# A hybrid encoder block on one core: six pairs instead of four by seven products, sums of weights on GpSimd, transposes in turns of eight

## The chip, the cores and the metric

The kernel runs on one core of a Trainium2 chip. The metric is the device time of one execution in microseconds (us), the median of some runs. Engines are named as in the profile: PE is the matrix engine (PEld its weight loads), DVE the vector engine, ACT the scalar engine, POOL is GpSimd, SP issues most DMAs.

## The reference

One encoder layer over 256 tokens of 2048 features, all in float32:

```python
h = rms_norm(x, attn_norm)
qa, ka, va, qb, kb, vb, ga, gb = split(h @ w_in)
ya = windowed_gqa(qa, ka, va, table, sink)         # 8 heads, |i-j| <= 128
yb = dilated_attention(qb, kb, vb, table)          # 3 groups of 4 heads
merged = sigmoid(ga) * (ya @ w_branch_a) + sigmoid(gb) * (yb @ w_branch_b)
x = x + merged @ w_out
hf = rms_norm(x, ffn_norm)
g = dwconv_centred(hf @ w_ffn_gate, conv_w, conv_b)  # width 3 along the tokens
x = x + (gelu(g) * (hf @ w_ffn_up)) @ w_ffn_down     # 5632 wide
x = x + sigmoid(rms_norm(x, ple_norm) @ w_ple_gate) * (p @ w_ple_proj)
return rms_norm(x, final_norm)
```

## The kernel before, in words

**Numbers.** A float32 factor is split into two parts that PE takes at full speed: `hi`, a rounded copy (ACT), and `lo`, the rest (DVE, a subtraction). A product is then three matmuls, hi by hi, hi by lo and lo by hi. For weights this is done in `split_to` (L205): a sub-piece of `raw` becomes `whi` (L217) and `wlo` (L218), four buffers each, and each product asks for splits three sub-pieces ahead of its own.

**Weights.** `_plan` lists the jobs, `_stream` the 128x128 weight blocks in the order in which the jobs use them. They lie in memory in pieces of 16 blocks (1 MB), which SP loads one after the other into three `raw` buffers (`load`, L195). A load waits until the piece three before it has been split.

**Stages.** Attention projections and attention; `ga`, `gb`, `ba`, `bb` (gates and branch projections) by quarters of the columns; `o` (`w_out`); then twice, for each half of the 5632 MLP features, `g` and `u` (gate and up projection, by 128 features) and `d0` or `d1` (down projection); `pp` and `pg` (the embedding and its gate), and the last norm. Accumulators lie in PSUM under the tags `acc` (three buffers), `sp`, `pt` (two each) and `misc`.

**The down projection.** A half has 22 blocks of 128 features, taken as 11 pairs. A product covers 1024 columns, so a pair has a 2x2 block matrix of activations (two features blocks by two token halves) and one of weights (two feature blocks by two column halves of 512). Eight small products would do; `seven_product` (L288) does the first `SAVED` pairs by seven, after Winograd's form of Strassen's scheme. Each small product is three matmuls of 512 columns (L311 to L313). `ORDER` mixes pairs by seven with pairs by eight. The seven need sums of weights, `combine` (L222, three DVE subtractions per piece of weights, L229, L233, L234, into the tile `spare`), and sums of activations, `add_up` (L704), made once for all `SAVED` pairs of a half into `shl`. A piece of a pair by seven is split in four parts: two blocks of raw, two of sums. When the last pair by seven is through, `spread_sums` (L721) adds the products `p1`, `p5`, `p6`, `p7` to the residual; the others are added at the end of the product by `joined` (L772).

**Transposes.** Activations are transposed on PE into a `pt` tile, four 128x128 transposes per tile, between the matmuls of another job: `merge` (L761) for the merged branches, `flip` (L740) after `w_out` and after `d1`. `at((job, step), f, ...)` names the place, and `run_due` runs it there.

**The end.** `finish` (L795) sums the squares of a token half (L798), takes the root (`root`, L384: a scaling on DVE and a power on POOL), and scales and stores the rows.

**What sets the order.** Each engine has its own queue in order. The order in a queue is that of a planner in the framework, which goes by the program's order as priority and by its own estimate of when an instruction can run; it also makes all semaphores.

Of the kernel before, what the change touches and what calls it, by code (L numbers as in the profile page):

```python
# [16 lines left out]
P = 128  # L17
T = 256
# [92 lines left out]

ORDER = [4, 0, 5, 1, 6, 2, 7, 3, 8, 9, 10]
SAVED = 4

# [43 lines left out]
def _encoder(ctx: ExitStack, tc, xt, pt, cols, table, onehot, mask, ident_in, last_gain, wts, xrows, out):  # L158
# [32 lines left out]

    raws, subs = {}, {}
    state = {"raw": 0, "sub": 0, "at": 0}

    def load(r, a=0, b=PIECE):  # L195
        if a == 0:
            raws[r] = wpool.tile([P, PIECE, P], F32, name="raw", bufs=3)
        nc.sync.dma_start(raws[r][:, a:b, :], wts[r].rearrange("p (b n) -> p b n", n=P)[:, a:b, :])
        state["raw"] = r + 1
# [5 lines left out]
    def split_to(i):  # L205
        while state["sub"] < min(i, len(_SUBS)):
            s = state["sub"]
            a, n, part = _SUBS[s]
            r, o = divmod(a, PIECE)
            load_all(r + 3)  # L210
            src = raws[r][:, o:o + n, :]
            if part is not None:
                src = combine(src, part)
                n = src.shape[1]
            hi = wpool.tile([P, n, P], FR, name="whi", bufs=4)
            lo = wpool.tile([P, n, P], FR, name="wlo", bufs=4)
            nc.scalar.activation(hi, src, AF.Copy)  # L217
            nc.vector.tensor_tensor(lo, src, hi.bitcast(F32), op=ALU.subtract)  # L218
            subs[s] = (hi, lo)
            state["sub"] = s + 1  # L220

    def combine(b, part):  # L222

        if part == 0:
            state["turn"] = turn = 1 - state.get("turn", 1)
            state["t"] = held["spare"][:, turn * PIECE * P:(turn + 1) * PIECE * P].rearrange("p (b n) -> p b n", n=P)
            four = b.rearrange("p (q b) n -> p q (b n)", q=4)
            t13 = state["t"][:, :8, :].rearrange("p (q b) n -> p q (b n)", q=2)
            nc.vector.tensor_tensor(t13, four[:, 1::2], four[:, :2], op=ALU.subtract)  # L229
            return b[:, 8:, :]  # L230
        if part == 1:
            t1, t2, t4 = (state["t"][:, c:c + 4, :] for c in (0, 8, 12))
            nc.vector.tensor_tensor(t2, b[:, 12:, :], t1, op=ALU.subtract)  # L233
            nc.vector.tensor_tensor(t4, b[:, 8:12, :], t2, op=ALU.subtract)  # L234
            return state["t"][:, :8, :]
        return state["t"][:, 8:, :] if part == 2 else b[:, :4, :]

# [50 lines left out]
    def seven_product(i, still, sums, tags, done):  # L288
# [30 lines left out]
        for m in ORDER:  # L319
            b = state["at"]  # L320
            s, _ = _SUB_OF[b]
            if m < SAVED:
                each = ([("p3", sums(m, 3), 0, 4), ("p2", a(2 * m + 1, 0), 0, 0)],
                        [("p5", sums(m, 0), 1, 0), ("p7", sums(m, 2), 1, 4)],
                        [("p6", sums(m, 1), 2, 0), ("p4", a(2 * m + 1, 1), 2, 4)],
                        [("p1", a(2 * m, 0), 3, 0)])
# [109 lines left out]
    tot = sc.tile([P, T], F32, name="tot")  # L436
    hba = big.tile([P, QH, AW], F32, name="hba", tag="b0", bufs=1)
    hbb = big.tile([P, BH, BW], F32, name="hbb", tag="b1", bufs=1)
    oh = ap_.tile([NBUCK, 2 * T], F32, name="oh", tag="near", bufs=2)
# [184 lines left out]
    def after(job, i, acc, u=None):  # L624
# [66 lines left out]
        elif kind == "u":  # L691
            u = gather(acc)
            nc.vector.scalar_tensor_tensor(u, u, 0.5, rt[1], op0=ALU.mult, op1=ALU.mult)
            f = n % FHALF
            v = held["a32"][:, f, :] if f < 2 * SAVED else u
# [8 lines left out]
    def add_up():  # L704

        a = held["a32"].rearrange("p (m e) (t n) -> p m e t n", e=2, t=2)
        a11, a12, a21, a22 = a[:, :, 0, 0], a[:, :, 1, 0], a[:, :, 0, 1], a[:, :, 1, 1]
        s = held["s32"]
        nc.vector.tensor_tensor(s[:, 0], a21, a22, op=ALU.add)
        nc.vector.tensor_tensor(s[:, 1], s[:, 0], a11, op=ALU.subtract)  # L710
        nc.vector.tensor_tensor(s[:, 2], a11, a21, op=ALU.subtract)
        nc.vector.tensor_tensor(s[:, 3], a12, s[:, 1], op=ALU.subtract)
        hi, lo = held["shl"][:, 0], held["shl"][:, 1]
        for c in (slice(0, 2), slice(2, 4)):
            nc.scalar.activation(hi[:, c], s[:, c], AF.Copy)
            nc.vector.tensor_tensor(lo[:, c], s[:, c], hi[:, c].bitcast(F32), op=ALU.subtract)

# [3 lines left out]
    def spread_sums(n, bank):  # L721
# [14 lines left out]
        add(v, bank["p5"], v)  # L736
        add(q[0][1], u, q[0][1])
        add(q[1][1], v, q[1][1])

# [21 lines left out]
    def merge(n, e, m):  # L761
# [5 lines left out]
        k = 4 * n + 2 * e  # L767
        hi, lo = (held["merged"][k // SUB][:, k % SUB:k % SUB + 2, c:c + T] for c in (0, T))
        nc.scalar.activation(hi, p, AF.Copy)
# [13 lines left out]
    def gate(n, t, acc, last):  # L783
# [9 lines left out]
        return u  # L793

    def finish(t, tail):  # L795

        s = sc.tile([P, 2], F32, name="sum")[:, :1]
        nc.vector.tensor_reduce(s, held["ss3"][:, t, :], axis=AX.X, op=ALU.add)  # L798
        r = root(s, 1)
        whole = res[:, t, :]  # L800
# [10 lines left out]
    def fetch(t, c):  # L811
# [8 lines left out]
    stills = {  # L820
        "o": lambda k: held["merged"][k // SUB][:, k % SUB, :], "ba": lambda k: yab[:, k, :],
        "bb": lambda k: yab[:, QH + k, :], "pp": lambda k: held["ps"][:, k, :], "pg": lambda k: held["pl"][:, k, :],
# [4 lines left out]
    for i, job in enumerate(_JOBS):  # L827
# [4 lines left out]
        if kind == "gb" and n == 0:  # L832
            held["merged"] = [big.tile([P, SUB, 2 * T], FR, name="merged", tag=a, bufs=1) for a in ("b0", "b1")]
        if kind == "o" and n == 0:
# [7 lines left out]
        if kind == "g" and n == 0:  # L842
            spare = held["spare"] = big.tile([P, KC * T], F32, name="spare", tag="b0", bufs=1)
            held["a32"] = spare[:, :2 * SAVED * T].rearrange("p (k t) -> p k t", t=T)
            held["s32"] = spare[:, 2 * SAVED * T:4 * SAVED * T].rearrange("p (e m n) -> p e m n", e=4, n=P)
            held["shl"] = big.tile([P, 2, 4, SAVED, P], FR, name="shl", tag="b1", bufs=1)
# [14 lines left out]
        if kind == "bb":  # L861
            for e in range(2):
                at((i + 1, 3 + 3 * e), merge, n, e, held["m"])
        if kind == "o":
            for e, j in enumerate(((i + 1, 2), (i + 1, 4)) if n < QUARTERS - 1 else ((i + 1, 9), (i + 1, 11))):
                at(j, flip, 4 * n + 2 * e, held["hf"], 1)
        if kind == "d1":
            for e, j in enumerate(((i + 2, 0), (i + 3, 0), (i + 3, 1), (i + 4, 1)) if n else
                                  [(i + 1, k) for k in (17, 18, 19, 20)]):
                at(j, flip, 8 * n + 2 * e, held["pl"], 2)  # L870
        if kind == "pp" and n == 0:
            end = ff.tile([P, 3 * QUARTERS, W4], F32, name="end", tag="act")
            held["ph"] = end[:, :2 * QUARTERS].rearrange("p (t n) w -> p t n w", t=2)
            held["lg"] = end[:, 2 * QUARTERS:].rearrange("p n w -> p (n w)")
        if kind == "pp" and n == 2:
            keep(nc.scalar.dma_start(held["lg"], last_gain))
            nc.vector.tensor_scalar(held["half"], root(rowsums(held["ss2"]), 2), 0.5, None, op0=ALU.mult)
# [48 lines left out]
        elif kind == "pg":  # L926
            for t in range(2):
# [3 lines left out]
                if last:  # L931
                    finish(t, tail)
        else:
            after(job, i, acc)
# [49 lines left out]
```

## Time and profile before

| | us |
|---|---|
| median of 3 runs (1477.53 to 1480.88) | 1478.37 |
| the profiled execution | 1477.88 |
| its span, first to last instruction | 1476.1 |
| PE busy | 1462.2 |
| DVE busy | 1065.5 |
| ACT busy | 760.5 |
| POOL busy | 3.7 |

The profile is one execution. Busy time is the time in which an engine had an instruction under way; in groups, "busy, mean ns of one" stands before the second bar, and after it the idle time of the engine just before these instructions, with what ended it. Matmuls overlap each other, so their mean duration is longer than their pitch.

### The profile page before, as it was taken

What the parts mean: (1) busy time and instruction counts of PE and PEld (TensorE: products, weight loads), DVE (VectorE), ACT (ScalarE), POOL (GpSimd) and SP (SyncE); (2) the same over time, 40 slices, a digit from 0 to 9 for tenths busy, and PEclk for the clock granted to TensorE, in tenths of its full rate; (3) what the DMA queues carried; (4) which work ended last, traced back from release to release, by engine and by line L of the source; (5) the groups of instructions that cost most, each with busy time, mean ns of one, the idle gap of its engine ahead of it and who ended that gap; (6) DMA issues with size and microseconds to landing.
All of it is one profiled execution on the core that took longest, in us unless ns stands there. A gap on an engine that the chain in (4) does not pass through costs nothing. (4 is left out here: it accounts for less than half of the span.)

```text
span 1476.1 us, 19530 instructions
## 1 busy us (share of the span) xinstructions
PE 1462.2 (99%) x7570; PEld 1248.4 (85%) x7570; DVE 1065.5 (72%) x1530; ACT 760.5 (52%) x1072; POOL 3.7 (0%) x9
## 2 busy tenths in 40 slices
PE   9999999999999999999999999999999999999997
PEld 8888888888888888888888888888888888888886
DVE  7686664664554555568898888887889888898565
ACT  7465444444444444555555555554555555655643
POOL 0000000000000000000000000000000000000000
PEclk9999999999999999999999999999999999999998
DMA  9644444445555554545455454555455454555552
GB/s 321 245 156 171 169 171 171 171 177 194 204 197 192 202 207 180 198 171 197 178 196 196 180 196 171 205 223 192 183 196 189 184 198 172 201 200 216 211 188 97
DMA packets 46375, 282.88 MB, mean 192 GB/s; under 512 B 5124, under 2 KB 9988, under 8 KB 14028
## 3 DMA queue, kind: packets, MB, share of 16 engines
q1 hardware_dynamic: 44268, 277.31, 50.8%
q10 hardware_dynamic: 2016, 4.33, 1.1%
q8 instruction: 59, 0.97, 0.2%
q14 instruction: 32, 0.26, 0.0%
HBM read 279.49 MB, written 2.14 MB: 191 GB/s over the span
## 5 line engine op out<-in xcount | busy, mean ns | idle before, releaser
L218 DVE TENSOR_TENSOR wlo<-raw,whi 128x1024 fp32r<-128x1024 f32 (+2 forms) x519 | 622.1, 1201 | 355.6 <-ACT whi L217 352.4
L217 ACT ACTIVATE whi<-raw 128x1024 fp32r<-128x1024 f32 (+2 forms) x519 | 541.1, 1043 | 605.5 <-PE acc L269 224.9
L244 PE MATMUL acc<-mov,whi 128*128 128x512 f32 x1840 | 641.9, 393 | 0.3 <-DVE mov L368 0.3
L245 PE MATMUL acc<-mov,wlo 128*128 128x256 f32 x1840 | 512.8, 279 | 0.0
L244 PEld LDWEIGHTS acc<-mov,whi 128*128 128x128 f32 x1840 | 344.7, 187 | 77.6 <-DVE mov L368 0.6
L245 PEld LDWEIGHTS acc<-mov,wlo 128*128 128x128 f32 x1840 | 346.7, 188 | 0.4
L268 PE MATMUL acc<-wlo,mov 128*128 128x512 f32 (+1 forms) x512 | 196.5, 384 | 0.5 <-DVE wlo L218 0.5
L267 PE MATMUL acc<-whi,mov 128*128 128x512 f32 (+1 forms) x512 | 196.8, 385 | 0.0
L269 PE MATMUL acc<-whi,mov 128*128 128x512 f32 (+1 forms) x512 | 196.4, 384 | 0.0
L267 PEld LDWEIGHTS acc<-whi,mov 128*128 128x128 f32 x512 | 96.7, 189 | 19.3 <-DVE wlo L218 0.8
L268 PEld LDWEIGHTS acc<-wlo,mov 128*128 128x128 f32 x512 | 96.7, 189 | 19.0 <-DVE wlo L218 0.9
L269 PEld LDWEIGHTS acc<-whi,mov 128*128 128x128 f32 x512 | 96.7, 189 | 18.8
L312 PE MATMUL acc<-wlo,act 128*128 128x512 f32 x272 | 106.3, 391 | 0.8 <-DVE wlo L218 0.8
L311 PE MATMUL acc<-whi,act 128*128 128x512 f32 x272 | 106.1, 390 | 0.0
L313 PE MATMUL acc<-whi,act 128*128 128x512 f32 x272 | 105.9, 389 | 0.0
L312 PEld LDWEIGHTS acc<-wlo,act 128*128 128x128 f32 x272 | 51.1, 188 | 12.0 <-DVE wlo L218 1.7
L311 PEld LDWEIGHTS acc<-whi,act 128*128 128x128 f32 x272 | 51.1, 188 | 10.7
L313 PEld LDWEIGHTS acc<-whi,act 128*128 128x128 f32 x272 | 51.1, 188 | 10.5
L267 PE MATMUL acc<-whi,merged 128*128 128x512 f32 x128 | 50.6, 396 | 0.0
L269 PE MATMUL acc<-whi,merged 128*128 128x512 f32 x128 | 49.9, 390 | 0.0
L268 PE MATMUL acc<-wlo,merged 128*128 128x512 f32 x128 | 49.8, 389 | 0.0
L217 ACT ACTIVATE whi<-spare 128x1024 fp32r<-128x1024 f32 x32 | 33.7, 1054 | 27.0 <-PE acc L313 26.2
(177 smaller groups left out, 1373.0 us busy)
## 6 DMA issues: line engine op xcount, KB each, us to landing
raw<-in_wts SPq DMA_DIRECT2D x251, 1024.0 KB, 4.8
raw<-in_wts SPq DMA_DIRECT2D x12, 512.0 KB, 7.4
x<-in_xrows ACTq DMA_DIRECT2D x8, 256.0 KB, 5.3
x<-in_xt SPq DMA_DIRECT2D x13, 128.0 KB, 6.6
hbb<-hold SPq DMA_DIRECT2D x3, 514.0 KB, 6.3
hba<-hold SPq DMA_DIRECT2D x2, 768.0 KB, 7.1
end<-in_last_gain ACTq DMA_DIRECT2D x1, 1024.0 KB, 4.8
out<-x ACTq DMA_DIRECT2D x2, 384.0 KB
```

The lines of the kernel that those rows point to most:

```text
L217: nc.scalar.activation(hi, src, AF.Copy)
L218: nc.vector.tensor_tensor(lo, src, hi.bitcast(F32), op=ALU.subtract)
L244: nc.tensor.matmul(acc, hi[:, o, :], m, start=first, stop=False, skip_group_check=True)
L245: nc.tensor.matmul(acc[:, T:], lo[:, o, :], m[:, :T], start=False, stop=last, skip_group_check=True)
L267: nc.tensor.matmul(acc, xh, hi, start=(k == 0), stop=False)
L268: nc.tensor.matmul(acc, xh, lo, start=False, stop=False)
L269: nc.tensor.matmul(acc, xl, hi, start=False, stop=(k == n - 1))
L311: nc.tensor.matmul(acc, xh, hi, start=(e == 1), stop=False)
L312: nc.tensor.matmul(acc, xh, lo, start=False, stop=False)
L313: nc.tensor.matmul(acc, xl, hi, start=False, stop=(e == uses[name]))
```

## The change

`SAVED` becomes 6 and `ORDER` is rewritten. In the second row of a pair by seven the column halves are stored in turned order, so that two neighbouring quarters of a piece can be added in one instruction. `combine` is replaced by `add_quarters`, three additions on GpSimd per piece, issued when the first part of the piece before is split; they go into two tiles, `ta` and `tb`. The signs are chosen so that the weights need additions only; `add_up` and `spread_sums` take up the signs. `add_up` is called for each pair as soon as both of its blocks are there. The two bias tiles become one (`hb`), and the tile `merged` is cut in 4 and 12 blocks instead of 8 and 8. Merges and most flips come two at a time. The last sum of squares is begun a quarter early (`so_far`), with its scale moved into the gain row.

```diff
-ORDER = [4, 0, 5, 1, 6, 2, 7, 3, 8, 9, 10]
-SAVED = 4
+ORDER = [6, 0, 7, 1, 2, 8, 3, 4, 5, 9, 10]
+SAVED = 6
+SPLIT = 4
...
-                blocks += [(name, k0 + 2 * m + e, c) for e in range(2) for c in n]
+                for e in range(2):
+                    turned = n[4:] + n[:4] if e and m < SAVED else n
+                    blocks += [(name, k0 + 2 * m + e, c) for c in turned]
...
             load_all(r + 3)
+            if (r + 1) * PIECE in _SEVEN and r + 1 not in both:
+                both[r + 1] = add_quarters(raws[r + 1])
             src = raws[r][:, o:o + n, :]
             if part is not None:
-                src = combine(src, part)
+                src = (src[:, 8:, :], both[r][:, :8, :], both[r][:, 8:, :], src[:, :4, :])[part]
...
-    def combine(b, part):
...
+    def add_quarters(b):
+        turn = state["turn"] = 1 - state.get("turn", 1)
+        t = held["spare"][turn]
+        nc.gpsimd.tensor_tensor(t[:, :8, :], b[:, :8, :], b[:, 4:12, :], op=ALU.add)
+        nc.gpsimd.tensor_tensor(t[:, 8:12, :], b[:, 8:12, :], t[:, :4, :], op=ALU.add)
+        nc.gpsimd.tensor_tensor(t[:, 12:, :], b[:, 12:, :], t[:, 8:12, :], op=ALU.add)
+        return t
...
-            if f == 2 * SAVED - 1:
-                add_up()
+            if f < 2 * SAVED and f % 2:
+                add_up(f // 2)
...
+    def add_up(m):
+        (a11, a21), (a12, a22) = [[held["two"][:, e, h] for h in HALVES] for e in range(2)]
+        s = held["ff"].tile([P, 4, P], F32, name="s32")
+        nc.vector.tensor_tensor(s[:, 0], a22, a21, op=ALU.subtract)
+        nc.vector.scalar_tensor_tensor(s[:, 1], s[:, 0], -1.0, a11, op0=ALU.mult, op1=ALU.subtract)
         nc.vector.tensor_tensor(s[:, 2], a11, a21, op=ALU.subtract)
+        nc.vector.tensor_tensor(s[:, 3], a12, s[:, 1], op=ALU.add)
+        hi, lo = (held["shl"][:, c, :, m, :] for c in range(2))
+        nc.scalar.activation(hi, s, AF.Copy)
+        nc.vector.tensor_tensor(lo, s, hi.bitcast(F32), op=ALU.subtract)
...
+    def so_far():
+        e = held["early"] = sc.tile([P, 2], F32, name="sum")
+        nc.vector.tensor_reduce(e, held["ss3"][:, :, :QUARTERS - 1], axis=AX.X, op=ALU.add)
+        nc.vector.tensor_scalar(e, e, D * EPS, None, op0=ALU.add)
...
-        nc.vector.tensor_reduce(s, held["ss3"][:, t, :], axis=AX.X, op=ALU.add)
-        r = root(s, 1)
+        nc.vector.tensor_tensor(v, held["ss3"][:, t, QUARTERS - 1:], held["early"][:, t:t + 1], op=ALU.add)
+        nc.gpsimd.tensor_tensor(r, v, mhalf[:, :1], op=ALU.pow)
...
-                at((i + 1, 3 + 3 * e), merge, n, e, held["m"])
+                at((i + 1, 4), merge, n, e, held["m"])
         if kind == "o":
-            for e, j in enumerate(((i + 1, 2), (i + 1, 4)) if n < QUARTERS - 1 else ((i + 1, 9), (i + 1, 11))):
+            for e, j in enumerate(((i + 1, 3), (i + 1, 3)) if n < QUARTERS - 1 else ((i + 1, 9), (i + 1, 11))):
...
-            for e, j in enumerate(((i + 2, 0), (i + 3, 0), (i + 3, 1), (i + 4, 1)) if n else
-                                  [(i + 1, k) for k in (17, 18, 19, 20)]):
+            for e, j in enumerate([(i + 2, 0), (i + 2, 0), (i + 3, 1), (i + 3, 1)] if n else
+                                  [(i + 1, k) for k in (17, 17, 19, 19)]):
...
+        if kind == "pp" and n == 3:
+            nc.vector.tensor_scalar(held["lg"], held["lg"], math.sqrt(D), None, op0=ALU.mult)
```

More of the change, by code (lines that the diff above doesn't have):

```diff
@@ L189, in _encoder @@
     sinks = cl[:, 4 * KC + 4 * FC:]
-    raws, subs = {}, {}
+    raws, subs, both = {}, {}, {}
     state = {"raw": 0, "sub": 0, "at": 0}
@@ L197, in load @@
             raws[r] = wpool.tile([P, PIECE, P], F32, name="raw", bufs=3)
-        nc.sync.dma_start(raws[r][:, a:b, :], wts[r].rearrange("p (b n) -> p b n", n=P)[:, a:b, :])
+        src = wts[r].rearrange("p (b n) -> p b n", n=P)
+        nc.sync.dma_start(raws[r][:, a:b, :], src[:, a:b, :])
         state["raw"] = r + 1
@@ L220, in split_to @@
             state["sub"] = s + 1
-    def combine(b, part):
[L224 to L236, printed above, removed]
+    def add_quarters(b):
[5 more added lines that the diff above has]
+        return t
     def block(acc, m, first, last, ahead=3):
@@ L322, in seven_product @@
             if m < SAVED:
-                each = ([("p3", sums(m, 3), 0, 4), ("p2", a(2 * m + 1, 0), 0, 0)],
+                each = ([("p3", sums(m, 3), 0, 0), ("p2", a(2 * m + 1, 0), 0, 4)],
                         [("p5", sums(m, 0), 1, 0), ("p7", sums(m, 2), 1, 4)],
@@ L436, in _encoder @@
     tot = sc.tile([P, T], F32, name="tot")
-    hba = big.tile([P, QH, AW], F32, name="hba", tag="b0", bufs=1)
-    hbb = big.tile([P, BH, BW], F32, name="hbb", tag="b1", bufs=1)
+    hb = big.tile([P, QH * AW + BH * BW], F32, name="hb", tag="b1", bufs=1)
+    hba = hb[:, :QH * AW].rearrange("p (h n) -> p h n", h=QH)
+    hbb = hb[:, QH * AW:].rearrange("p (h n) -> p h n", h=BH)
     oh = ap_.tile([NBUCK, 2 * T], F32, name="oh", tag="near", bufs=2)
@@ L694, in after @@
             f = n % FHALF
-            v = held["a32"][:, f, :] if f < 2 * SAVED else u
+            if f < 2 * SAVED:
+                if f % 2 == 0:
+                    held["two"] = ff.tile([P, 2, T], F32, name="two")
+                v = held["two"][:, f % 2, :]
+            else:
+                v = u
             nc.vector.tensor_tensor(v, u, held.pop(("gelu", n)), op=ALU.mult)
             halves(held["act"][:, f, :], v)
-            if f == 2 * SAVED - 1:
-                add_up()
+            if f < 2 * SAVED and f % 2:
+                add_up(f // 2)
         elif kind == "pp":
@@ L736, in spread_sums @@
         add(v, bank["p5"], v)
-        add(q[0][1], u, q[0][1])
-        add(q[1][1], v, q[1][1])
+        for dst, a in ((q[0][1], u), (q[1][1], v)):
+            nc.vector.tensor_tensor(dst, dst, a, op=ALU.subtract)
     def flip(n, dst, norm):
@@ L767, in merge @@
         k = 4 * n + 2 * e
-        hi, lo = (held["merged"][k // SUB][:, k % SUB:k % SUB + 2, c:c + T] for c in (0, T))
+        part, k = (held["merged"][k >= SPLIT], k - SPLIT * (k >= SPLIT))
+        hi, lo = (part[:, k:k + 2, c:c + T] for c in (0, T))
         nc.scalar.activation(hi, p, AF.Copy)
@@ L793, in gate @@
         return u
+    def so_far():
+        e = held["early"] = sc.tile([P, 2], F32, name="sum")
+        nc.vector.tensor_reduce(e, held["ss3"][:, :, :QUARTERS - 1], axis=AX.X, op=ALU.add)
+        nc.vector.tensor_scalar(e, e, D * EPS, None, op0=ALU.add)
     def finish(t, tail):
-        s = sc.tile([P, 2], F32, name="sum")[:, :1]
-        nc.vector.tensor_reduce(s, held["ss3"][:, t, :], axis=AX.X, op=ALU.add)
-        r = root(s, 1)
+        r = sc.tile([P, 1], F32, name="rr", bufs=3)
+        v = sc.tile([P, 1], F32, name="rv", bufs=3)
+        nc.vector.tensor_tensor(v, held["ss3"][:, t, QUARTERS - 1:], held["early"][:, t:t + 1], op=ALU.add)
+        nc.gpsimd.tensor_tensor(r, v, mhalf[:, :1], op=ALU.pow)
         whole = res[:, t, :]
@@ L820, in _encoder @@
     stills = {
-        "o": lambda k: held["merged"][k // SUB][:, k % SUB, :], "ba": lambda k: yab[:, k, :],
+        "o": lambda k: held["merged"][k >= SPLIT][:, k - SPLIT * (k >= SPLIT), :], "ba": lambda k: yab[:, k, :],
         "bb": lambda k: yab[:, QH + k, :], "pp": lambda k: held["ps"][:, k, :], "pg": lambda k: held["pl"][:, k, :],
@@ L832, in _encoder @@
         if kind == "gb" and n == 0:
-            held["merged"] = [big.tile([P, SUB, 2 * T], FR, name="merged", tag=a, bufs=1) for a in ("b0", "b1")]
+            held["merged"] = [big.tile([P, k, 2 * T], FR, name="merged", tag=a, bufs=1)
+                              for a, k in (("b0", SPLIT), ("b1", KC - SPLIT))]
         if kind == "o" and n == 0:
@@ L842, in _encoder @@
         if kind == "g" and n == 0:
-            spare = held["spare"] = big.tile([P, KC * T], F32, name="spare", tag="b0", bufs=1)
-            held["a32"] = spare[:, :2 * SAVED * T].rearrange("p (k t) -> p k t", t=T)
-            held["s32"] = spare[:, 2 * SAVED * T:4 * SAVED * T].rearrange("p (e m n) -> p e m n", e=4, n=P)
+            held["spare"] = [big.tile([P, PIECE, P], F32, name="ta", tag="b0", bufs=1),
+                             ff.tile([P, PIECE, P], F32, name="tb")]
             held["shl"] = big.tile([P, 2, 4, SAVED, P], FR, name="shl", tag="b1", bufs=1)
@@ L932, in _encoder @@
                     finish(t, tail)
+            if n == QUARTERS - 2:
+                so_far()
         else:
```

11 lines of the change are left out of this document (removed).

## The prediction

> **What bounds the kernel now.** I read the page's engine line first, then the groups by line, the stages of the down projection (windows), the waits, and the timelines of PE around the places that the change touches.
>
> ```profile
> PE 1462.2 (99%) x7570; PEld 1248.4 (85%) x7570; DVE 1065.5 (72%) x1530; ACT 760.5 (52%) x1072; POOL 3.7 (0%) x9
> ```
>
> PE is busy for 1462.2 of 1476.1 us and POOL does next to nothing. A busy PE could still be a slow PE, so the stage that is changed comes next: `seven_product`, four products (two halves of the MLP by two halves of the columns), each of eleven pieces, four of them pairs by seven.
>
> ```profile
> core 0: us, PE busy (x) PEld busy (x) DVE busy (x) ACT busy (x) POOL busy (x), PEclk, DMA share, GB/s
> 643.00:888.00 245.00, 244.73 (x1414) 215.57 (x1413) 206.23 (x364) 129.18 (x204) 0.71 (x1) 1.00 0.51 187
> 888.90:946.30 57.40, 56.97 (x252) 46.84 (x251) 50.03 (x57) 30.87 (x33) 0.00 (x0) 1.00 0.55 202
> 946.30:1003.70 57.40, 57.02 (x252) 46.90 (x251) 47.90 (x53) 30.19 (x31) 0.00 (x0) 1.00 0.54 202
> 1250.00:1307.40 57.40, 57.40 (x255) 47.54 (x254) 50.77 (x58) 31.04 (x34) 0.00 (x0) 1.00 0.56 209
> 1307.40:1364.90 57.50, 57.50 (x263) 47.29 (x262) 49.36 (x57) 35.34 (x48) 0.00 (x0) 1.00 0.51 192
> ```
>
> The first row is a gate/up half, the other four are the products. In each PE is full at a granted clock of 1.00 with 252 matmuls (4 pairs of 21, 7 of 24), and DVE works about 50 of 57.4 us. Whoever takes matmuls away gains their pitch, as long as DVE, now second, is not pushed past PE.
>
> ```profile
> L311 PE MATMUL acc<-whi,act 128*128 128x512 f32 x272 | 106.1, 390 | 0.0
> L311 PE MATMUL acc<-whi,shl 128*128 128x512 f32 x64 | 24.9, 389 | 0.0
> ...
> 896.28 0.39 PE L313 MATMUL acc<-whi,shl 128*128 128x512 f32 x1
> ...
> 902.40 0.39 PE L313 MATMUL acc<-whi,act 128*128 128x512 f32 x1
> ...
> ACT whi L217 <- PE acc L313: 94.9, 95, 2.1
> ...
> PE acc L312 <- DVE wlo L218: 0.8, 2, 0.4
> ```
>
> A matmul's 390 ns overlap the next one's: from 896.28 to 902.40 there are 27 starts, so the pitch is 6.12/27 = 0.2267 us. A piece of a pair by seven takes 21 of them, 4.76 us, one by eight 24, 5.44 us. The two waits say who leads: ACT waits for PE to give back weight buffers (94.9 us), and PE waits for a split only 0.8 us in all. Splits run ahead, by three of the four buffers `whi`/`wlo`. Three parts of a seven-piece are 18 matmuls, 4.1 us: that is the cushion.
>
> **The change, part by part.**
>
> *Matmuls.* Two more pairs by seven, in four products: 2 x 4 x 3 = 24 matmuls of 0.2267 us, **-5.4 us**. This is on PE's path. The products shrink from 57.1 to 55.8 us (6 x 4.76 + 5 x 5.44).
>
> *Sums of weights.* The DVE instructions of `combine` go, and three POOL additions per piece come, of the same sizes.
>
> ```profile
> L218 DVE TENSOR_TENSOR wlo<-spare,whi 128x1024 fp32r<-128x1024 f32 x32 | 39.1, 1222 | 11.4 <-ACT whi L217 11.1
> L229 DVE TENSOR_TENSOR spare<-raw 128x1024 f32<-128x1024 f32 x16 | 19.5, 1221 | 4.1 <-DMA raw<-in_wts 3.9
> L234 DVE TENSOR_TENSOR spare<-raw,spare 128x512 f32<-128x512 f32 x16 | 11.0, 689 | 0.3
> L233 DVE TENSOR_TENSOR spare<-raw,spare 128x512 f32<-128x512 f32 x16 | 11.0, 685 | 0.0
> L389 POOL TENSOR_TENSOR rr<-rv,mhalf 128x2 f32<-128x2 f32 (+2 forms) x5 | 3.5, 706 | 1466.5 <-DVE rv L387 1466.5
> ...
> L728 DVE TENSOR_TENSOR x<-sq,x 128x512 f32<-128x512 f32 x8 | 5.5, 684 | 0.0
> L776 DVE TENSOR_TENSOR x<-acc,x 128x512 f32<-128x512 f32 x16 | 10.1, 684 | 1.8 <-PE acc L313 1.8
> ```
>
> On DVE a seven-piece keeps three splits of 1.22 and one of 0.68, 4.34 us, and loses 1.22 + 0.69 + 0.69 = 2.6. A product then costs DVE 6 x 4.34 + 5 x 2.44 = 38.2 of splits, 8 x 0.68 of `spread_sums` and 4 x 0.68 of `joined`: 46.4 of 55.8 us, where it was 50 of 57.4. DVE gets slack.
>
> What POOL's additions cost the trace does not show: its work here is roots on one to four elements. Lower bound: DVE's own 2.6 us per piece. Upper bound: POOL's smallest root takes 0.56 us where DVE's smallest instructions take 0.16 (both rows stand below, in the tail), 3.5 times, so 9.1. I take the geometric middle, 4.9 us. [...]
>
> At 4.9 this is hidden. `add_quarters` for piece r+1 is issued when the first part of piece r is split, and its raw has landed about then, since a raw's buffer is free one piece earlier. New waits: ACT's `whi` and DVE's `wlo` of parts 1 and 2 wait for POOL, and behind them in their queues stand the later splits, `spread_sums` and `joined`. POOL's own queue holds otherwise only the five roots, none in these stages. SP's loads stay the same pieces in the same order. The tightest place is pairs 3, 4, 5 in a row: from the landing of piece 3's raw to the split of piece 5's part 2 there are 5.44 + 2 x 4.76 + 2.7 = 17.7 us, and 21.8 with the cushion. Three sums of 4.9 are 14.7. Cost **0**; the cover ends at 7.2 us per piece.
>
> *Sums of activations* move into the up projection, pair by pair.
>
> ```profile
> L716 DVE TENSOR_TENSOR shl<-spare,shl 128x1024 fp32r<-128x1024 f32 x4 | 4.7, 1219 | 0.0
> L397 DVE TENSOR_SCALAR rdg<-ident,rr 128x128 f32<-128x128 f32 x4 | 1.0, 282 | 2.0 <-POOL rr L389 2.0
> ```
>
> Before, a half had four 512-wide sums and two splits of 1.22: 5.2 us of DVE. Now each pair has four of 128 columns (0.28 each) and one 512 split: 1.8, so 10.9 a half. 5.7 us more in a stage with 206 of 245 us is hidden; uncovered it would be 11 us in all. DVE also waits each time for ACT's `hi`, under 1 us, ahead of the next weight split, which is within the cushion.
>
> *Turns of eight transposes.* Merges, `w_out` flips and last flips are paired: 4 + 3 + 4 = 11 turns fewer.
>
> ```profile
> 577.24 0.39 PE L269 MATMUL acc<-whi,merged 128*128 128x512 f32 x1
> 577.47 0.60 PE L745 MATMUL pt<-ident,x 128*128 128x128 f32 x4
> ...
> 580.46 0.39 PE L269 MATMUL acc<-whi,merged 128*128 128x512 f32 x1
> ...
> L745 PE MATMUL pt<-ident,x 128*128 128x128 f32 x64 | 9.6, 272 | 0.0
> ```
>
> Between the two L269 lie 12 wide pitches, 2.72 of 3.22 us, so a turn of four costs 0.50. Its transposes start (0.60 - 0.27)/3 = 0.11 apart, so four more in the same turn cost 0.44. Saved: 11 x 0.06, **-0.7 us**. Both `pt` buffers must be free at once, else the second four come later, as now.
>
> *The tail.*
>
> ```profile
> 1469.41 0.16 DVE L798 TENSOR_REDUCE sum<-marks 128x1 f32<-128x4 f32 x1
> 1469.60 0.16 DVE L387 TENSOR_SCALAR rv<-sum 128x1 f32<-128x1 f32 x1
> 1469.90 0.56 POOL L389 TENSOR_TENSOR rr<-rv,mhalf 128x1 f32<-128x1 f32 x1 [4.85 <-DVE rv L387]
> ```
>
> Two DVE instructions become one ahead of the last root: 1469.60 - 1469.41, **-0.2 us**. `so_far` lies under the last quarter.
>
> *End of the second half.* Here two things get worse. `spread_sums` comes two pairs before the end of the product instead of three, and the gain row is multiplied on DVE (2048 wide; by L806 of the tail, 0.61 us for 768, 1.6 us) behind its own DMA.
>
> ```profile
> 1382.00 0.50 PE L268 MATMUL acc<-wlo,mov 128*128 128x512 f32 x1 [0.52 <-DVE wlo L218]
> ...
> L368 DVE SCALAR_TENSOR_TENSOR mov<-pt,cl,mov 128x256 fp32r<-128x256 f32 x32 | 14.9, 479 | 5.5 <-ACT mov L367 5.3
> ...
> 1470.89 0.61 DVE L806 TENSOR_SCALAR x<-x,rr 128x768 f32<-128x768 f32 x1
> ```
>
> PE already stalls about 0.5 us here behind a split. Earlier flips may end that (-0.5), and the multiplication may add its whole 1.6. I take the middle, **+0.5**.
>
> Signs in `spread_sums`, the joint tile `hb`, and 4 + 12 blocks of `merged` change no count on PE's path: **0**.
>
> Sum: -5.4 - 0.7 - 0.2 + 0.5 = **-5.8 us**. The profiled execution took 1477.88 us (span 1476.1 and 1.8 around it) and would take 1472.1; it lies 0.5 below the median of 1478.37, so I forecast **1472.6**, its own range 1470 to 1476.
>
> **The rivals.**
>
> *POOL and DVE take turns on SBUF (slower).* If no DVE instruction with both inputs in SBUF runs while POOL adds, a product has 38.2 of splits, 2.7 of the four SBUF-only adds of `spread_sums` and 6 x 4.9 of POOL in series: 70.3 against 55.8 us. Two products in a row give 29.0 over, less the cushion of 4.1, twice: 50 us, **1522**. At POOL's lower bound of 2.6 the sum is 56.5 and costs almost nothing; it decides from 2.5 us per piece that DVE can't use. The trace is silent: POOL's five roots ran while DVE waited for them. Against it: if even half of POOL's time left DVE running, 40.9 + 14.7 = 55.6 would fit. Chance 0.27. [...]
>
> *POOL is slow by itself, or slowed.* Above 7.2 us per piece the sums of 3, 4, 5 come late; at 9.1, 3 x 9.1 - 21.8 = 5.5 us in each of four products, 22 us, up to **1495**, about 1486 in the middle. Then DVE's `wlo` would wait for POOL, and DVE would be idle rather than busy. Chance 0.15.
>
> *The gain goes at the end of the second half.* From `spread_sums` to the end of the product DVE has 5.5 of sums, 8 x 0.48 of flips and four splits: 14.2 us in 10.9 (it was 16.6 in 16.3). The cushion of 4.1 holds the missing 3.3 only if it is full after three seven-pieces; empty, it is +3.3, and with the gain row's 1.6 undiminished about +4.4: **1476 to 1477**. Chance 0.10.
>
> **How the numbers follow.** Forecast 0.48, rivals 0.27, 0.15, 0.10. A measurement of this kernel can tell about 0.2% (3 us) from no change. Faster: the forecast and a tenth of the third rival, 0.49. Same: most of the third and a little of the second, 0.08. Slower: 0.43. The range runs from the forecast's low end, 1470, past the second rival to **1512**: it leaves out 0.02 below and about 0.17 above, the upper part of the first rival.
>
> **What would show it.** Right: L311 counts fall from 336 to 328, products of 55.8 us, DVE's 128x1024 splits still 1.22 us while POOL adds, PE's idle time before the act products under 2 us, POOL near 24 x 4.9 = 118 us. Wrong: splits of 2 us or more, or DVE and POOL strictly alternating (first rival); `wlo` or `whi` waiting for POOL and PE for `wlo` in pairs 4 and 5 (second); a PE gap just after the last product (third).

## The result, and the profile after

The changed kernel takes 1523.75 us (median of 4 runs, 1523.26 to 1524.12), the kernel before 1479.39 beside it (4 runs, 1477.53 to 1480.88): 1.030 times as long, 95% interval 1.0282 to 1.0318. The prediction was 1472.6, range 1470 to 1512. The profiled execution took 1523.7 us, 45.8 more than that of before.

The page of the changed kernel, its engine line and POOL's costliest group:

```profile
PE 1478.0 (97%) x7546; PEld 1242.1 (82%) x7546; DVE 1148.2 (75%) x1547; ACT 773.6 (51%) x1096; POOL 163.8 (11%) x81
...
L233 POOL TENSOR_TENSOR ta<-raw 128x1024 f32<-128x1024 f32 x12 | 34.8, 2901 | 534.9 <-DMA raw<-in_wts 520.6
```

PE has 24 matmuls fewer (7570 before), yet 15.8 us more busy time: the last matmul before a stall counts with its whole 0.39 us instead of its pitch, some after a stall last up to 0.79, and the pitch itself has grown in places (e4, below). POOL's 72 additions take 160.4 of its 163.8 us, 6.7 per piece. Where the time lies is told by the stages, each from the first matmul of a product to that of the next, or to the end of its last (profiled executions):

| from | to | before, us | after, us |
|---|---|---|---|
| start | first product | 889.0 | 892.5 |
| four products | | 57.9, 58.0, 57.1, 59.4 | 68.1, 68.5, 67.8, 70.0 |
| between the halves | | 244.4 | 245.3 |
| after the last product | | 110.3 | 109.8 |

So 42.0 us are in the products, 3.5 lie ahead of the first one. The windows of the changed kernel over the four products:

```profile
core 0: us, PE busy (x) PEld busy (x) DVE busy (x) ACT busy (x) POOL busy (x), PEclk, DMA share, GB/s
892.20:960.40 68.20, 60.70 (x249) 46.48 (x248) 66.69 (x50) 34.58 (x40) 37.65 (x18) 0.97 0.46 170
960.40:1028.80 68.40, 60.21 (x248) 45.30 (x246) 67.50 (x50) 33.30 (x35) 36.20 (x16) 1.00 0.48 171
1274.10:1341.90 67.80, 60.16 (x248) 45.39 (x248) 66.58 (x51) 34.69 (x40) 39.14 (x18) 1.00 0.46 171
1341.90:1411.90 70.00, 62.24 (x264) 46.94 (x263) 68.23 (x54) 38.96 (x51) 36.06 (x16) 1.00 0.46 165
```

DVE, the third of the busy times behind the duration, is now busy for 66.7 of 68.2 us where it was about 50 of 57.4, although it has fewer instructions. Some of its instructions must last longer; the groups by shape say which:

```profile
L224 DVE TENSOR_TENSOR wlo<-raw,whi 128x1024 fp32r<-128x1024 f32 x490 | 627.3, 1283 | 331.4 <-ACT whi L223 330.6
L224 DVE TENSOR_TENSOR wlo<-tb,whi 128x1024 fp32r<-128x1024 f32 x24 | 48.7, 2045 | 2.9 <-ACT whi L223 2.7
L224 DVE TENSOR_TENSOR wlo<-ta,whi 128x1024 fp32r<-128x1024 f32 x24 | 45.5, 1927 | 0.3 <-ACT whi L223 0.3
L224 DVE TENSOR_TENSOR wlo<-raw,whi 128x512 fp32r<-128x512 f32 x26 | 30.8, 1186 | 0.7 <-ACT whi L223 0.7
L732 DVE TENSOR_TENSOR sq<-acc,sq 128x512 f32<-128x512 f32 x8 | 5.5, 688 | 0.1
```

A split of 1024 columns was 1.22 us; those of the sums now last 1.9 to 2.0 on average, and one of 512 went from 0.69 to 1.19. `sq<-acc,sq`, with one of its two inputs in PSUM, kept its 0.69. The waits name who is late:

```profile
PEld acc L312 <- DVE wlo L224: 48.9, 41, 2.8
PE acc L312 <- DVE wlo L224: 30.8, 31, 2.4
...
ACT whi L223 <- POOL tb L235: 13.5, 4, 3.4
...
ACT whi L223 <- POOL ta L235: 6.8, 4, 2.9
```

PE waits for DVE's splits 31 times, 30.8 us in all (0.8 before); ACT waits for POOL's sums only 8 times. The timelines of POOL and DVE, side by side at two places, show why the splits are long (start, duration):

```profile
883.10 2.99 POOL L233 TENSOR_TENSOR ta<-raw 128x1024 f32<-128x1024 f32 x1 [232.70 <-DMA raw<-in_wts]
886.16 1.37 POOL L234 TENSOR_TENSOR ta<-raw,ta 128x512 f32<-128x512 f32 x1
...
955.33 2.40 POOL L233 TENSOR_TENSOR ta<-raw 128x1024 f32<-128x1024 f32 x1 [14.23 <-DVE gate L732]
957.82 1.63 POOL L234 TENSOR_TENSOR ta<-raw,ta 128x512 f32<-128x512 f32 x1
```

```profile
884.20 2.18 DVE L680 TENSOR_TENSOR u<-u,rms 128x256 f32<-128x256 f32 x1
886.41 1.27 DVE L682 TENSOR_SCALAR c<-u,cl 128x256 f32<-128x256 f32 x1
...
955.36 0.69 DVE L732 TENSOR_TENSOR sq<-acc,sq 128x512 f32<-128x512 f32 x1
955.97 2.32 DVE L732 TENSOR_TENSOR x<-gate,x 128x512 f32<-128x512 f32 x1
958.21 1.78 DVE L742 TENSOR_TENSOR x<-x,sq 128x512 f32<-128x512 f32 x1
```

At 955.36 DVE reads one input from PSUM and runs its 0.69 us beside POOL. At 955.97 both inputs are in SBUF, the on-chip memory that holds the tiles (PSUM holds the accumulators of PE): an instruction of 0.68 us lasts 2.32, and ends at 958.29, 0.56 after POOL's addition ended at 957.73. POOL's next addition, issued at 957.82, ends only at 959.45, 1.16 after DVE was done, and DVE's next one ends 0.54 after that. They take turns, one instruction each. Through the whole trace a 1024-column split that comes while an addition runs ends 1.08 us after the addition's end (46 splits, median; 8 others came first and kept their 1.22), and POOL's additions end 2.26 us (1024 columns) and 1.15 us (512) after the DVE instruction before them, in the median. I take these as POOL's own durations, an estimate, since the shortest additions recorded are 2.39 and 1.29 us. A piece is then 2.26 + 1.15 + 1.15 = **4.56 us** of POOL alone.

That makes the sum. Per product DVE has 38.2 + 2.7 = 40.9 us of instructions with two SBUF inputs (the first rival's terms), and POOL 6 x 4.56 = 27.4 in series with them: 68.3 us, and the products measure 68.1, 68.5, 67.8 and 70.0. The turns are shown; that the sum agrees to 0.2 us is partly luck, for two of its errors pull in opposite ways: a held split adds 1.08 us and not 1.22, and the eight instructions with an input in PSUM, 0.68 us each, are left out although DVE has only 1 to 2 us idle per product.

### The profile page after: what moved, and what is told of

It reads as the page before. It is cut to its first block, busy times and chain, and to the rows that moved or that the text cites. A ratio compares the mean times of both kernels' runs of the same rounds, so it can differ in the third digit from the quotient of the medians.

```text
span 1521.9 us, 19683 instructions
## 1 busy us (share of the span) xinstructions
PE 1478.0 (97%) x7546; PEld 1242.1 (82%) x7546; DVE 1148.2 (75%) x1547; ACT 773.6 (51%) x1096; POOL 163.8 (11%) x81
## 4 chain that ended last, share of the span: by engine, by line
PE 80%; DVE 12%; issue 4%; ACT 1%; POOL 1%; DMA 1%; SPq 0%; POOLq 0%; DVEq 0%; ACTq 0%
PE acc L244 26%; PE acc L245 13%; PE acc L267 11%; PE acc L269 11%; PE acc L268 11%; DVE wlo L224 8%; PE first L244 1%; PE acc L312 1%; DMA raw<-in_wts 1%; ACT whi L223 1%; PE acc L313 1%; PE acc L311 1%; PE first L245 1%; PE pt L581 0%; POOL tb L233 0%
## 5 line engine op out<-in xcount | busy, mean ns | idle before, releaser
L224 DVE TENSOR_TENSOR wlo<-raw,whi 128x1024 fp32r<-128x1024 f32 (+2 forms) x519 | 657.9, 1274 | 335.5 <-ACT whi L223 334.7
L312 PE MATMUL acc<-wlo,act 128*128 128x512 f32 x232 | 93.3, 402 | 5.5 <-DVE wlo L224 5.3
L233 POOL TENSOR_TENSOR ta<-raw 128x1024 f32<-128x1024 f32 x12 | 34.8, 2901 | 534.9 <-DMA raw<-in_wts 520.6
L313 PE MATMUL acc<-whi,act 128*128 128x512 f32 x232 | 91.8, 396 | 0.0
L311 PE MATMUL acc<-whi,act 128*128 128x512 f32 x232 | 91.8, 395 | 0.0
L312 PE MATMUL acc<-wlo,shl 128*128 128x512 f32 x96 | 41.0, 427 | 25.6 <-DVE wlo L224 25.6
L312 PEld LDWEIGHTS acc<-wlo,act 128*128 128x128 f32 x232 | 43.6, 188 | 21.3 <-DVE wlo L224 11.6
L311 PEld LDWEIGHTS acc<-whi,act 128*128 128x128 f32 x232 | 43.6, 188 | 10.3
L313 PEld LDWEIGHTS acc<-whi,act 128*128 128x128 f32 x232 | 43.6, 188 | 9.7
L312 PEld LDWEIGHTS acc<-wlo,shl 128*128 128x128 f32 x96 | 18.4, 191 | 40.6 <-DVE wlo L224 37.3
```

Source lines behind the costliest of these rows:

```text
L233: nc.gpsimd.tensor_tensor(t[:, :8, :], b[:, :8, :], b[:, 4:12, :], op=ALU.add)
L311: nc.tensor.matmul(acc, xh, hi, start=(e == 1), stop=False)
L312: nc.tensor.matmul(acc, xh, lo, start=False, stop=False)
L313: nc.tensor.matmul(acc, xl, hi, start=False, stop=(e == uses[name]))
```

## The experiments

All times are medians, ratios against the kernel before on the same chip (1478.4 to 1478.7 us). "Products" are the four durations as in the table above, of the profiled execution. The theory: DVE and POOL take turns on SBUF. Rivals: POOL's sums come late; POOL's mere activity, or its writes, cost the time; the other edits of the change do.

**e1_unread: POOL adds, nobody reads.**

```diff
-                src = (src[:, 8:, :], both[r][:, :8, :], both[r][:, 8:, :], src[:, :4, :])[part]
+                src = (src[:, 8:, :], src[:, :8, :], src[:, 8:, :], src[:, :4, :])[part]
```

> The changed kernel, but nobody reads GpSimd's sums: the parts are split from raw blocks of the same size, so the seven products get wrong weights (left out: the sums of weights). GpSimd still adds 24 times. Theory, turns on SBUF: DVE is held up as before although nobody waits for a sum; products stay near 68 us, splits that meet an addition keep about 2 us, total 1517 to 1524. Rival, sums come too late: with no one waiting the products fall to 56 or 57 us and the total to about 1482 (1479.4 - 5.4 - 0.2, and 3.4 + 4.7 for the longer matmul pitch in the yab and act stages of the changed kernel).

1525.2 us, ratio 1.031 (1.0295 to 1.0326), products 68.0, 68.8, 67.9, 70.2. With no sum to wait for, nothing is won: lateness of the sums is out. The splits are held though none of them reads a sum (0.69 and 1.22 us in the kernel before; the means are over all stages):

```profile
L224 DVE TENSOR_TENSOR wlo<-raw,whi 128x1024 fp32r<-128x1024 f32 x538 | 716.8, 1340 | 341.3 <-ACT whi L223 340.2
L224 DVE TENSOR_TENSOR wlo<-raw,whi 128x512 fp32r<-128x512 f32 x26 | 27.1, 1043 | 1.7 <-ACT whi L223 1.7
```

**e2_memset: POOL writes, reads nothing.**

```diff
-        nc.gpsimd.tensor_tensor(t[:, :8, :], b[:, :8, :], b[:, 4:12, :], op=ALU.add)
...
+        for c in (slice(0, 8), slice(8, 12), slice(12, 16)):
+            for _ in range(4):
+                nc.gpsimd.memset(t[:, c, :], 0.5)
```

> The changed kernel with GpSimd's three additions per piece replaced by twelve memsets of the same three areas (four each), which write and read nothing; the sums of weights are left out, a constant stands there. All waits for the sums stay. Theory, turns on SBUF for reads: DVE's 128x1024 splits stay 1.22 us beside them, products 56 to 57 us, total about 1482. Rival, sums come too late: if the memsets of a piece take as long as the additions did (6.7 us), products stay near 68 us and the total near 1524. If GpSimd's writes hold DVE too, also near 1520.

1480.47 us, ratio 1.0013 (1.0003 to 1.0022), products 57.1, 57.3, 57.1, 59.1. Its groups by shape:

```profile
L235 POOL MEMSET ta<- 128x512 f32 (+1 forms) x144 | 91.0, 673 | 579.5 <-DVE wlo L224 517.0 <-PE acc L269 60.7
...
L224 DVE TENSOR_TENSOR wlo<-ta,whi 128x1024 fp32r<-128x1024 f32 x24 | 29.4, 1224 | 6.9 <-ACT whi L223 6.7
```

POOL is busy for 7.6 us per piece (91.0 and 90.9 us over 24 pieces), longer than the 6.7 of the stretched additions, and writes the same tiles four times over; the splits of 1024 columns keep their 1.22 us in every group (means of 1223 ns over 490 from `raw`, 1224 over 24 from `ta`, 1223 over 24 from `tb`), those of 512 their 0.69 (689 ns over 26). So neither POOL's activity nor its writes hold DVE; with the PSUM input that was not held, this points at POOL's reading of SBUF. No run had POOL compute without reading.

**e3_dve6: the sums on DVE.**

```diff
-        nc.gpsimd.tensor_tensor(t[:, :8, :], b[:, :8, :], b[:, 4:12, :], op=ALU.add)
+        nc.vector.tensor_tensor(t[:, :8, :], b[:, :8, :], b[:, 4:12, :], op=ALU.add)
...
```

> The changed kernel with the same three additions on DVE instead of GpSimd. Theory, turns on SBUF: an addition costs DVE 2.6 us a piece directly instead of 4.6 us in waiting; DVE per product 62.0 us by durations, some 58 us since its instructions overlap by about 7 percent (53.0 by durations was 50 busy in the kernel before); products about 58 us, total 1481 to 1487. Rival, something else in the change slows the products (order of pairs, sums of activations): stays above 1505.

1485.43 us, ratio 1.0047 (1.003 to 1.0063), products 57.2, 57.9, 57.3, 59.7. The products get 42 us back; what is left over 1479 lies outside them, 4.7 us ahead of the first product, 1.1 between the halves and 1.6 after the last one, where PE stands 2.0 us. The largest part, and the gap, are followed below.

**e4_align: where tiles lie.** The joint tile `hb` is 24,624 bytes long, and all tiles behind it moved by 64 bytes. The list of one tile's instructions, `yab` (stationary in the branch projections), first of the kernel before, then of the changed one (count, duration min/median/max):

```profile
L268 PE MATMUL acc<-wlo,yab x96: 389/389/389, 353.6 to 551.6; 128*128 128x512 f32 x96
```

```profile
L268 PE MATMUL acc<-wlo,yab x96: 393/396/398, 354.7 to 554.6; 128*128 128x512 f32 x96
```

The same matmul takes 7 ns longer, and from the first to the last start it is 199.9 us, not 198.0. Padding puts the tiles back where they were within 512 bytes:

```diff
-    hb = big.tile([P, QH * AW + BH * BW], F32, name="hb", tag="b1", bufs=1)
+    hb = big.tile([P, 49 * P], F32, name="hb", tag="b1", bufs=1)
```

> The changed kernel with the joint bias tile padded to 6272 columns, so that all tiles behind it lie 448 bytes higher, at the same offset modulo 512 bytes to the weight tiles as in the kernel before (they lie 64 bytes off in the changed kernel). Theory, placement: matmul pitch with yab and act back from 0.233 to 0.227 us, first act product about 3 us earlier, total 1520 to 1521 (the products stay bound by DVE). Rival, the pitch comes from the order of instructions: no change, 1523.7.

1520.79 us, ratio 1.0281 (1.0266 to 1.0296); the tile's matmuls are 389 ns again, the first product starts at 889.7 instead of 892.5. So the joint tile costs 3 us here, and more where PE is the bound: `act` is the stationary tile of 232 matmuls in each of the three lines of `seven_product`, with a pitch of 0.2333 us in the changed kernel against 0.2267 in the one before. What it costs there is read from e2 and e8 below.

**e5_dve6b, e6_dve5b, e7_dve4b, e8_memset_b.** All four have the padding, and multiply the gain row two steps later:

```diff
-        if kind == "pp" and n == 3:
-            nc.vector.tensor_scalar(held["lg"], held["lg"], math.sqrt(D), None, op0=ALU.mult)
+        if kind == "pg" and n == 0:
+            at((i, 6), lambda: nc.vector.tensor_scalar(held["lg"], held["lg"], math.sqrt(D), None, op0=ALU.mult))
```

e5 has six pairs with the sums on DVE as in e3, e8 six with the memsets of e2. e6 has five pairs and e7 four, in the order of before, both with the sums on DVE:

```diff
-ORDER = [6, 0, 7, 1, 2, 8, 3, 4, 5, 9, 10]
-SAVED = 6
+ORDER = [5, 0, 6, 1, 7, 2, 3, 8, 4, 9, 10]   # e7: [4, 0, 5, 1, 6, 2, 7, 3, 8, 9, 10]
+SAVED = 5                                    # e7: 4
```

> Six pairs, sums on DVE, bias tile padded to 6272 columns, gain row multiplied in the middle of the first quarter of pg instead of before the last of pp. From 1485.4 of the unpadded one: 3.7 us less before the down projection, up to 4 x 1.4 in it (pitch 0.233 to 0.227), 2 at the gain row. If DVE has room for six pairs: products 55.8 us, total 1475 to 1477. If DVE is the bound at six pairs (some 58 us a product): products stay above 57, total 1479 to 1481.

> The same with five pairs by seven, ORDER 5, 0, 6, 1, 7, 2, 3, 8, 4, 9, 10. DVE has room (about 53 of 56.4 us). Four products of 56.4 us, 2.7 us less than the kernel before in all, and 0.5 for turns and tail: 1475.2. If the six-pair kernel is faster than this one, DVE was not the bound there.

> The same with four pairs by seven in the order of the kernel before: all the rest of the change without the two more pairs and without GpSimd. Turns of eight and the tail give 0.3 + 0.2 us: 1477.9, the same as before within the noise. If the rest costs something by itself: above 1480.

> Six pairs, memsets on GpSimd in place of the additions (the sums of weights are left out), padded tile, gain row later: the forecast's own terms without GpSimd's reads. Products 55.8 us; 1478.4 - 5.4 - 0.5 = 1472.5 if the terms of the sum were right, 1478 or more if the matmuls taken away do not shorten the products.

| | us (range) | ratio, 95% | products |
|---|---|---|---|
| e5, six | 1480.06 (1477.77 to 1486.41) | 1.0012 (1.0004 to 1.0021) | 56.4, 57.7, 56.4, 58.9 |
| e6, five | 1474.99 (1473.97 to 1475.96) | 0.9977 (0.9968 to 0.9986) | 56.5, 56.6, 56.5, 58.9 |
| e7, four | 1477.47 (1476.56 to 1480.92) | 0.9997 (0.9988 to 1.0005) | 57.2, 58.3, 57.1, 59.3 |
| e8, six, memsets | 1471.49 (1470.85 to 1471.97) | 0.9953 (0.9941 to 0.9965) | 55.8, 55.9, 55.8, 57.9 |

e8 is the forecast's kernel with sums that cost nothing, but with the padding and the later gain row: 1471.49 against the forecast 1472.6, products of 55.8 as worked out. e2, the same memsets without padding, took 1480.47, with products of 57.1. So with the joint tile as written the forecast gain would not have come even if POOL's sums had cost nothing: the tile's place takes 9.0 us by these medians (7.1 between the profiled executions, 2.0 of it ahead of the first product and 5.3 in the products), and the later gain row hardly counts, since both spend 109.6 to 109.7 us after the last product. e7, four pairs with the padding and the sums on DVE, shows no difference to the kernel before that can be told. e6 beats it by 3.4 us. e5's total lies where its expectation put DVE as the bound (1479 to 1481), but partly for another reason, since two of its products take 56.4 us: it loses 3.1 us after the last product. Its timeline of DVE there:

```profile
1378.19 1.23 DVE L888 TENSOR_SCALAR end<-end 128x2048 f32<-128x2048 f32 x1 [3.87 <-DMA end<-in_last_gain]
1379.33 0.87 DVE L368 SCALAR_TENSOR_TENSOR mov<-pt,cl,mov 128x256 fp32r<-128x256 f32 x2
```

The planner put the gain row's multiplication ahead of the flips' `mov`; DVE stands 3.87 us for the row's DMA, and PE stands 3.65 us behind it, until the `mov` is there.

**e9_pool5b, e10_pool4b: fewer pairs, sums on POOL.** e6 and e7 with the sums back on GpSimd:

```diff
-        nc.vector.tensor_tensor(t[:, :8, :], b[:, :8, :], b[:, 4:12, :], op=ALU.add)
+        nc.gpsimd.tensor_tensor(t[:, :8, :], b[:, :8, :], b[:, 4:12, :], op=ALU.add)
...
```

> Five pairs by seven with the sums on GpSimd, otherwise as e6_dve5b (bias tile padded, gain row multiplied later). Turns on SBUF: per product 5 x 4.34 + 6 x 2.44 = 36.3 of splits, 2.7 of sums with both inputs in SBUF and 5 x 4.56 of GpSimd in series, 61.8 us, where PE takes 56.5: products of about 61.8 us, 4 x 5.3 = 21 us over e6_dve5b, about 1496. If GpSimd only came late, or slowed DVE by a share, five pairs would be as e6_dve5b, 1475, with products of 56.5.

> Four pairs with the order of before and the sums on GpSimd, otherwise as e7_dve4b. Turns: 4 x 4.34 + 7 x 2.44 + 2.7 + 4 x 4.56 = 55.4 us in series, under PE's 57.1: PE stays the bound, about 1478 as e7_dve4b (1477.5), products of 57 to 58.5 us, and the additions still stretched. A rival by which each addition costs PE a wait of its own would leave +2 us per pair, 16 pairs: 1495 or more.

e9: 1501.65 us, ratio 1.0152 (1.0138 to 1.0166). e10: 1486.54 us, ratio 1.0053 (1.0037 to 1.0068), products 60.2, 59.0, 60.2, 61.4. The windows of e9, and a short one in its last product:

```profile
888.40:950.40 62.00, 58.90 (x251) 46.06 (x250) 58.68 (x47) 32.99 (x38) 31.46 (x14) 1.00 0.51 187
950.40:1014.20 63.80, 59.19 (x251) 46.04 (x249) 61.66 (x49) 31.74 (x33) 29.42 (x14) 1.00 0.50 181
1260.40:1322.40 62.00, 58.88 (x252) 46.03 (x251) 58.71 (x48) 32.98 (x38) 30.84 (x14) 1.00 0.51 187
1322.40:1389.70 67.30, 63.23 (x267) 49.91 (x266) 63.88 (x53) 37.53 (x49) 29.74 (x14) 0.95 0.47 172
1332.00:1338.90 6.90, 6.00 (x14) 4.75 (x15) 6.90 (x5) 3.21 (x4) 4.12 (x2) 0.51 0.12 26
```

Two products take 62.0 us where turns give 61.8; the rival's 56.5 is out. The second takes 63.8, and the last 67.3, 5.3 more than the first; 2.4 of that is there in e6 too (58.9 against 56.5). In the last, PE stood 3.1 us for a split, and from within that stall 6.8 us passed at a granted clock of 0.50. So the total missed by 5 to 6 us, and the first and third product did not.

e10 missed by 8.5 us, some 2 per product. The sum per product, 55.4, is under PE's 57.1, but the time isn't spread evenly: in the first eight pieces, four pairs and four others in turn, the turns need 4 x (4.34 + 4.56 + 2.44) = 45.4 us, and PE 4 x (4.76 + 5.44) = 40.8. The idle time of DVE at the end of a product can't be used for that. That would be 4.6 us, and the first and third product lost 3.1 against 57.1; no run tested this reading apart. The price per pair that e10's expectation set as a rival, 2 us, would have given 1495 and is out.

**e11_dve6c, e12_dve5c: the gain row held in place.** e5 and e6, with the multiplication kept in program order, behind the first flips.

```diff
-            at((i, 6), lambda: nc.vector.tensor_scalar(held["lg"], held["lg"], math.sqrt(D), None, op0=ALU.mult))
+            at((i, 6), lambda: keep(nc.vector.tensor_scalar(held["lg"], held["lg"], math.sqrt(D), None, op0=ALU.mult)))
```

> e5_dve6b (six pairs, sums on DVE), with the gain row's multiplication held at its place in the order, behind the first flips of the last job. If the gap of 3.9 us after the last product was that multiplication waiting for its own DMA, it goes: 1480.1 - 3.7 = about 1476.4. If the gap was the flips themselves, 1480 stays.

> e6_dve5b (five pairs, sums on DVE), with the gain row's multiplication held in the same way. It did not wait there: 1474.9, as before, within 0.5 us. If it hid a wait, up to 1 us less.

e11: 1476.39 us (1475.75 to 1480.93), ratio 0.9987 (0.9978 to 0.9996). e12: 1474.42 us (1473.94 to 1475.01), ratio 0.9969 (0.9957 to 0.998). Both as expected: in e11 the wait is gone and the multiplication lies 5 us later,

```profile
1383.43 1.22 DVE L888 TENSOR_SCALAR end<-end 128x2048 f32<-128x2048 f32 x1
```

and the 3.7 us came back by the medians (2.7 between the two profiled executions). e12 and e6 are the best whole kernels found; their intervals overlap. Why five pairs beat six on DVE is read from e11's windows over its first two products, and e12's:

```profile
887.90:944.40 56.50, 56.48 (x249) 46.04 (x248) 54.62 (x64) 34.03 (x37) 0.00 (x0) 1.00 0.56 203
944.40:1001.70 57.30, 56.68 (x248) 45.85 (x246) 57.07 (x65) 33.48 (x35) 0.00 (x0) 1.00 0.55 202
```

```profile
889.20:945.70 56.50, 56.50 (x252) 46.72 (x251) 51.48 (x60) 32.47 (x35) 0.00 (x0) 1.00 0.56 203
945.70:1002.30 56.60, 56.60 (x251) 46.71 (x249) 53.58 (x59) 31.78 (x33) 0.00 (x0) 1.00 0.57 206
```

With six pairs DVE is full in the second product (57.07 of 57.30 us), and PE, with fewer matmuls, is no faster; with five DVE still has 3 us. The order of the pairs differs between the two as well, and was not tried apart.

## Why the prediction was wrong

**The step that failed** is "Sums of weights ... At 4.9 this is hidden. Cost 0". The size was near, by luck, as the middle of bounds of 2.6 and 9.1: POOL alone takes 4.56 us per piece by the estimate above, taken as 4.9. What failed is that POOL's time would lie beside DVE's. The first rival, chance 0.27, had the mechanism, its place and nearly its time, 1522 against 1523.75. Against it the prediction had only "if even half of POOL's time left DVE running", with no row for such a half; the changed kernel, e1 and e9 show that DVE instructions with two SBUF inputs get no such share: one that meets an addition waits for its end (46 splits of the changed kernel end 1.08 us after it, in the median). The rival's own sizes are off in both directions: 4.9 was high by 0.34 a piece, 8.2 us in all, and the cushion of 4.1 us, taken off once per pair of products, another 8.2, did not show. That the two cancel is luck. The step "DVE gets slack" fell with it. It also set a sum of durations, 46.4, against a busy time, 50; the same sum for the kernel before is 53.0.

The runs show these turns part by part. A DVE instruction with two SBUF inputs that begins beside an addition lasts 2.32 us instead of 0.68 (changed kernel, 955.97); a split of 1024 columns keeps 1.22 in a stage where POOL only writes (e2); an instruction with one input in PSUM keeps 0.69 beside an addition (changed kernel, 955.36).

**Matmuls, -5.4**: right. e8's products take the 55.8 us worked out, and with the sums free it is 7.0 us below the kernel before. The total of e8 is near the forecast partly by luck: in the profiled executions its products save 6.9 us, 1.5 more than the matmuls, since two products of the kernel before took 0.8 us longer than 57.1, and 1.2 us are lost between the halves.

**Turns of eight, -0.7**: the sign holds, the size not quite. Over seven turns whose surroundings are alike, e4 saves 0.27 us, 0.04 a turn and not 0.06.

**The joint tile `hb`, 0**: wrong, and a second failed step. It moved tiles by 64 bytes and cost 3.0 us in e4; where PE is the bound it costs 7 to 9 (e2 against e8), more than the whole forecast gain of 5.8. It was hidden from the argument because only counts and order were weighed, not addresses.

**The sums of activations**, hidden: right. Window 643 to 888, DVE busy 209.3 us after, 206.2 before, PE as full as before:

```profile
643.00:888.00 245.00, 244.67 (x1409) 215.34 (x1408) 209.28 (x379) 130.14 (x207) 5.45 (x4) 1.00 0.53 189
```

**The tail, -0.2**: near. From the end of the last matmul to the end 9.67 us before, 9.37 after.

**End of the second half, +0.5**: in the changed kernel nothing is lost there (109.8 against 110.3). The multiplication took 1.23 us, not 1.6, and stood behind the flips. Where something was lost, in e3 and e5, the planner had put it ahead of the last flips, and the term was the wait for its DMA: 2.3 us in e3, 3.9 in e5. In e2, e6 and e8, with products as short, it stood behind the flips and cost nothing, so it was the order that counted. The third rival's place was right there, its cause was not: the row, not the cushion.

**End of the first half**, where the prediction has no term: here the later `spread_sums` does cost time. DVE comes late to the sums of `joined`, and PE waits for the first of them:

```profile
1028.93 2.48 DVE L781 TENSOR_TENSOR x<-acc,x 128x512 f32<-128x512 f32 x4
...
1029.76 0.47 PE L244 MATMUL acc<-mov,whi 128*128 128x512 f32 x1 [0.70 <-DVE x L781]
```

Between the halves the changed kernel takes 245.3 us instead of 244.4, and every run with five or six pairs 245.3 to 246.1; the two with four, e7 and e10, whose `spread_sums` comes three pairs before the end, take 244.4.

## What to carry to other kernels

Moving an elementwise step with operands in SBUF from DVE to GpSimd freed no time here, beside DVE's own instructions with two SBUF operands: the products took 67.8 to 70.0 us with the sums on GpSimd, 57.2 to 59.7 with the same sums on DVE (e3). Where two engines may take turns like this, add both times in one sum, per stretch and not only per stage, before believing that one hides the other. Fewer matmuls pay only as far as the engine that feeds them has room, so the best count is where both are just full (here, with the sums on DVE, five pairs, not four or six). When a tile changes its size, look at where the tiles behind it come to lie (64 bytes cost 3.0 us in e4); and an instruction that waits for a DMA belongs behind those that others wait for.

## What the runs showed of the hardware that was not expected

- DVE's `TENSOR_SCALAR` with one SBUF tensor (L682, 886.41 above) was held too: 1.27 us beside an addition, 0.41 for the shortest of its 44 in the changed kernel. L355, with one SBUF and one PSUM input, was not: 0.42 beside an addition (at 1265.67 us), 0.41 to 0.42 in all 100 of this form.
- The matmuls of 512 columns with `yab` or `act` as the stationary tile had a pitch of 0.2333 us in the changed kernel, where these tiles lie 64 bytes off, within 512, and 0.2267 in the kernel before. With the tiles put back (e4) those with `yab` lasted 389 ns again, 396 in the changed kernel. Which of the two operands' places counts was not tried.
- The granted clock fell to 0.50 for 6.8 us from within one stall of 3.1 us (e9), and in the changed kernel for 3.4 us after several shorter ones, the longest 2.35, that left PE busy 6.1 of the 9.6 us before. A second stall of 2.35 us, at 1317, did not lower it. Over the whole profiled span the mean granted clock was 0.992 in e1 and 0.993 in e4, 0.997 in the changed kernel. The lines are of the changed kernel:

```profile
929.60:939.20 9.60, 6.09 (x23) 3.64 (x21) 9.60 (x5) 3.70 (x4) 9.36 (x5) 1.00 0.28 109
939.20:942.60 3.40, 2.94 (x8) 2.10 (x7) 3.40 (x3) 1.06 (x1) 1.91 (x1) 0.50 0.00 0
```
